# Eight PSUM banks dealt out anew among dense sums, down products and norms in an inference step

## The chip, the cores and the metric

The kernel runs on one core of a Trainium2 chip. The metric is the device time of one execution in microseconds; the median of three executions before the change is 4295.14 (4291.89 to 4296.32). A separate execution was profiled, and its trace is what is read below.

## The reference

One inference step of a small hybrid diffusion backbone, width 1024, on 1280 token positions: 256 of one request's context (x_prompt) and 1024 of a noisy sample (x_sample). There are two trunk layers, each a mixer and an MLP, with a residual add behind each:

```
x = x + gate * mixer(rmsnorm(x) * (1 + scale) + shift)     # scale, shift, gate: linear in silu(c)
x = x + gate * (relu(h @ w1) ** 2) @ w2                    # h = rmsnorm(x) * (1 + scale) + shift
```

The even layer's mixer is a gated DeltaNet beside a short gated convolution; the odd layer's is a windowed attention with grouped queries and sink logits beside an RWKV-7 time mixing. Both mixers start with dense projections of h (some followed by a convolution of three taps) and end with a dense output projection. After the two layers a last RMSNorm gives y_prompt and y_sample; the final DeltaNet and RWKV states and the key and value cache of the context are outputs too.

## The kernel before

**Layout and precision.** x lies transposed in SBUF, eight tiles of 128 features by 1280 positions. Positions are worked in three chunks, `CHUNKS`, in this order: 512, 512 and 256 columns. Every float32 operand of a dense product is split into a high and a low part (`split`, L243 to L247, on ScalarE, VectorE or GpSimd), and a product is the sum of three matmuls: high by high, high by low, low by high. `dense_mm` (to L271) makes one dense sum of 128 output features by up to 512 positions: eight blocks of 128 inputs by three matmuls, 24 in all, added up in one PSUM tile.

**PSUM.** There are eight banks. `set_ps` (L99) closes the pools that are open and opens one pool for each keyword, in the order of the keywords, with as many tiles as the number says; `ps_t` (L104) takes a tile of 128x512 float32, one bank, from the pool of that name. `ps_d()` is a tile of pd (dense sums), `ps_m()` one of pm. A pool goes round its banks: a new tile waits until the last reader of the tile that had its bank is done. Pools are opened at five places:

- L138, for the load of x, the modulation vectors and the first norm
- L587, for the even mixer (pd dense sums, pm small products, pg and pr the DeltaNet's)
- L1293, for RWKV and attention (pc, pp, pi, pa, po), which has no pd and is not touched
- L1895, for the even mixer's output, the first MLP and the odd mixer's projections
- L1905, for the odd mixer's output, the second MLP and the final norm

**Who uses pd.** At the places with three pools: `load_x` (L456), which transposes x (L151) four blocks to a tile and copies them out on VectorE (L472) and ScalarE (L470); the MLP's up sums; the odd mixer's projections (`conv_block` and L1202 to L1250), emptied by ScalarE (L571 and L572 in `conv_block`, L1205 behind it); the output projections (L1054, L1859), emptied by VectorE into x; `final`, which transposes the result four blocks to a tile and empties it at L542 on VectorE.

**Who uses pn and pm.** A norm takes a pn tile for the sums of squares of a chunk (`rstd_chunk`: squares by ScalarE at L419 or GpSimd at L417, sums by TensorE at L421, read by VectorE at L424) and one to spread the result over the partitions (L440), which VectorE reads at L445; activations at L448 and L451 on ScalarE follow. `mod_vec` takes tiles for the modulation vectors, whose partial sums VectorE adds at L344 and L346. pm also holds the MLP's down products.

**The MLP** (`mlp`, L475) goes through 16 groups of 256 hidden features. `up` makes for each of the group's two blocks a dense sum (L271), a ReLU from PSUM on ScalarE (L495), a square (L496) and a split. `down` makes eight output blocks of six matmuls (L506 to L508) and adds them into x on VectorE (L509). Within a group:

```
h0 = up(a0, n0)        # 512 columns: two dense sums
h1 = up(a1, n1)        # 512 columns: two dense sums
down(h0, a0, n0, s0)
h2 = up(a2, n2)        # 256 columns: two dense sums
```

**What sets the order.** The Tile framework plans the program: each engine gets a static list of instructions, drawn up from program order, priorities (the sums of squares and the spreading of a norm stand under a high priority) and a simulated timeline. On the chip each engine works through its list in order, and an instruction that waits holds back all behind it on that engine, the transfers that the engine issues included.

Of the kernel before, what the change touches and what calls it, by code (L numbers as in the profile page):

```python
# [85 lines left out]
def tile_kernel(ctx, tc, I, O):  # L86
# [7 lines left out]
    def pool(es, name, bufs, **kw):  # L94
        return es.enter_context(tc.tile_pool(name=name, bufs=bufs, reuse_waits="tile", **kw))
# [3 lines left out]
    def set_ps(**banks):  # L99
        ps_es.close()  # L100
        for nm, n in banks.items():
            state[nm] = pool(ps_es, nm, n, space=PSUM)
# [30 lines left out]
    def open_t5(es, bufs, sq=0, **kw):  # L133
        state["t5"] = pool(es, "t5", bufs, **kw)
        if sq:
            state["sq"] = pool(es, "sq", sq, **kw)

    set_ps(pd=3, pm=3, pn=2)  # L138


    cnames, _, cnames64, _ = const_arrays()
# [95 lines left out]
    def open_w(es, nraw, nhl):  # L237
        state["raw"] = pool(es, "wraw", nraw)
        state["whl"] = pool(es, "whl", nhl)
# [338 lines left out]
    def even_mixer(hs):  # L578
# [5 lines left out]
        mid.update(o=sp_o, s=sp_s)  # L584
        tap = lambda k, j: vec["gdn_conv"][:, k * 12 + j:k * 12 + j + 1]
        stap = lambda k, j: vec["sc_conv"][:, k * 4 + j:k * 4 + j + 1]
        set_ps(pd=2, pm=1, pg=2, pr=3)  # L587
        with ExitStack() as es:
            cp = pool(es, "conv", 1, side="right")
            mp = pool(es, "modp", 2, side="right")  # L590
# [1300 lines left out]
    xes.close()  # L1891

    even_mixer(hs)

    set_ps(pd=3, pm=3, pn=2)  # L1895
    open_t5(tes, 4, 3, side="right")
    xt = new_x(xes)
    unspill_x(xt)
# [3 lines left out]
    mlp(wes, 0, xt, hs, mod_gate(0, 1), [(), ()] + [(1, 512 * n) for n in range(12)])  # L1902
    odd_mixer(xt, hs, hes, xes, wes)

    set_ps(pd=3, pm=3, pn=2)  # L1905
    open_w(wes, 2, 2)
    hs = new_h(hes)
    open_t5(tes, 4, 2, side="right")
# [42 lines left out]
```

## Time and profile before

| what | value |
|---|---|
| median of three runs | 4295.14 us (4291.89 to 4296.32) |
| profiled execution, its own time | 4296.43 us |
| its span | 4294.6 us |
| TensorE busy | 3989.5 us, 93% of the span |
| VectorE busy | 2240.2 us, 52% |
| ScalarE busy | 1269.8 us, 30% |
| GpSimd busy | 1279.6 us, 30% |
| matmuls | 27995 |

The span is from the first to the last instruction in the trace; the profiled execution's own time has a little around it. Busy time is the time in which an engine has an instruction in work. An idle time before an instruction is put down to the event that released it, and a TensorE instruction's length overlaps with that of the next, since matmuls are pipelined: the distance between two starts is what one costs.

The stages follow one another: load, modulation and first norm up to 120 us; the even mixer to about 905, with its output behind it; the first MLP from 982 to about 1905; norm and projections of the odd mixer to 2113; RWKV and attention from 2114 to 3195; the odd mixer's output from 3198 to 3347; the second MLP from 3348; the final norm to the end.

### The profile page before, as it was taken

What the parts mean: (1) busy time and instruction counts of PE and PEld (TensorE: products, weight loads), DVE (VectorE), ACT (ScalarE), POOL (GpSimd) and SP (SyncE); (2) the same over time, 40 slices, a digit from 0 to 9 for tenths busy, and PEclk for the clock granted to TensorE, in tenths of its full rate; (3) what the DMA queues carried; (4) which work ended last, traced back from release to release, by engine and by line L of the source; (5) the groups of instructions that cost most, each with busy time, mean ns of one, the idle gap of its engine ahead of it and who ended that gap; (6) DMA issues with size and microseconds to landing.
All of it is one profiled execution on the core that took longest, in us unless ns stands there. A gap on an engine that the chain in (4) does not pass through costs nothing.

```text
span 4294.6 us, 70066 instructions
## 1 busy us (share of the span) xinstructions
PE 3989.5 (93%) x27995; PEld 3293.4 (77%) x27995; DVE 2240.2 (52%) x4724; ACT 1269.8 (30%) x2691; POOL 1279.6 (30%) x1139
## 2 busy tenths in 40 slices
PE   7889989998999999999889889999859999999999
PEld 4777778787888888887667667776648888888888
DVE  2467676545455555453365577777631433333333
ACT  3554543222111111133223234444321311111111
POOL 1544542223222333232432231212022323223321
PEclk8989999999999999999989889999879999999999
DMA  5323332432122222125466543333241111111111
GB/s 198 103 82 102 95 97 73 128 124 72 54 75 71 73 77 74 47 87 188 144 211 183 140 104 90 94 91 86 53 144 47 30 40 40 40 40 40 40 35 54
DMA packets 437957, 382.98 MB, mean 89 GB/s; under 512 B 125684, under 2 KB 373503, under 8 KB 437503
## 3 DMA queue, kind: packets, MB, share of 16 engines
q1 hardware_dynamic: 403727, 310.34, 24.7%
q10 hardware_dynamic: 33904, 68.17, 4.8%
q8 instruction: 220, 3.60, 0.4%
q14 instruction: 106, 0.87, 0.1%
HBM read 290.31 MB, written 88.08 MB: 88 GB/s over the span
## 4 chain that ended last, share of the span: by engine, by line
PE 75%; DVE 11%; DMA 7%; issue 3%; ACT 2%; POOL 2%; SPq 1%; ACTq 0%; DVEq 0%; POOLq 0%
PE pd L271 31%; PE pm L506 7%; PE pm L507 7%; PE pm L508 7%; PE pd L280 3%; PE pn L421 2%; PE po L1453 1%; PE pa L1271 1%; PE pp L1583 1%; PE pa L1442 1%; DVE stmp L842 1%; DVE sub L844 1%; DMA modw<-in_mod_w_dram 1%; DMA hst<-sp_h 1%; DMA vg<-sp_k 1%
## 5 line engine op out<-in xcount | busy, mean ns | idle before, releaser
L271 PE MATMUL pd<-hhi,whl 128*128 128x512 f32 (+1 forms) x5376 | 1527.7, 364 | 45.4 <-ACT hhi L243 23.4
L271 PEld LDWEIGHTS pd<-hhi,whl 128*128 128x128 f32 x5376 | 966.8, 191 | 200.1 <-ACT hhi L243 24.7
L271 PE MATMUL pd<-hlo,whl 128*128 128x512 f32 (+1 forms) x2688 | 980.1, 365 | 10.9 <-POOL hlo L247 9.2
L509 DVE SCALAR_TENSOR_TENSOR x<-pm,mods,x 128x512 f32<-128x512 f32 (+1 forms) x768 | 502.4, 660 | 751.1 <-PE pm L508 751.0
L247 POOL TENSOR_TENSOR whl<-raw,whl 128x1024 fp32r<-128x1024 f32 (+2 forms) x203 | 469.6, 2323 | 605.0 <-ACT whl L243 605.0
L271 PEld LDWEIGHTS pd<-hlo,whl 128*128 128x128 f32 x2688 | 514.9, 192 | 90.8 <-POOL hlo L247 11.2
L506 PE MATMUL pm<-hh,whl 128*128 128x512 f32 (+1 forms) x1536 | 546.9, 356 | 0.0
L507 PE MATMUL pm<-hl,whl 128*128 128x512 f32 (+1 forms) x1536 | 545.1, 355 | 0.0
L508 PE MATMUL pm<-hh,whl 128*128 128x512 f32 (+1 forms) x1536 | 544.1, 354 | 0.0
L495 ACT ACTIVATE t<-pd 128x512 f32<-128x512 f32 (+1 forms) x192 | 100.9, 527 | 1311.9 <-PE pd L271 1311.9
L247 POOL TENSOR_TENSOR hl<-t,hh 128x512 fp32r<-128x512 f32 (+1 forms) x192 | 216.2, 1126 | 822.8 <-DVE hh L245 806.0
L506 PEld LDWEIGHTS pm<-hh,whl 128*128 128x128 f32 x1536 | 289.4, 188 | 44.5
L507 PEld LDWEIGHTS pm<-hl,whl 128*128 128x128 f32 x1536 | 289.8, 189 | 43.6
L508 PEld LDWEIGHTS pm<-hh,whl 128*128 128x128 f32 x1536 | 289.9, 189 | 41.6
L245 DVE CAST hh<-t 128x512 fp32r<-128x512 f32 (+1 forms) x192 | 166.6, 869 | 236.1 <-ACT t L496 235.9
L243 ACT ACTIVATE whl<-raw 128x1024 fp32r<-128x1024 f32 (+2 forms) x203 | 201.8, 1011 | 154.6 <-PE pm L508 75.0
L357 POOL TENSOR_TENSOR acc<-acc,modw 128x512 f32<-128x512 f32 x112 | 149.2, 1332 | 135.1 <-ACT modw L353 116.6
L346 DVE SCALAR_TENSOR_TENSOR acc<-modw,scp,acc 128x512 f32<-128x512 f32 x168 | 129.0, 804 | 3.8 <-DMA modw<-in_mod_w_dram 3.8
L1271 PE MATMUL pa<-hst,whl 128*128 128x512 f32 (+1 forms) x432 | 120.9, 380 | 9.2 <-DMA hst<-sp_h 8.7
L353 ACT ACTIVATE modw<-modw,scp 128x256 f32<-128x256 f32 x224 | 112.7, 506 | 54.6 <-DMA modw<-in_mod_w_dram 49.6
L421 PEld LDWEIGHTS pn<-cst,sq 128*128 128x128 f32 x800 | 109.3, 209 | 8.2 <-issue 2.5
L280 PE MATMUL pd<-hhi,whl 128*128 128x512 f32 (+1 forms) x384 | 111.5, 366 | 2.5 <-DVE xr L1015 1.6
(387 smaller groups left out, 6019.1 us busy)
## 6 DMA issues: line engine op xcount, KB each, us to landing
raw<-in_mlp_w_dram SPq DMA_DIRECT2D x128, 512.0 KB
modw<-in_mod_w_dram SPq DMA_DIRECT2D x112, 256.0 KB
hst<-sp_h ACTq DMA_DIRECT2D x48, 512.0 KB
modw<-in_mod_w_dram SPq DMA_DIRECT2D x128, 128.0 KB
rkk<-sp_r SPq DMA_DIRECT2D x40, 384.0 KB
raw<-in_ev_w_in_dram SPq DMA_DIRECT2D x28, 512.0 KB
x_dram<-x SPq DMA_DIRECT2D x16, 640.0 KB
x<-x_dram ACTq DMA_DIRECT2D x32, 256.0 KB
```

What stands on the lines that cost most here:

```text
L243: A.activation(out=hi, in_=src, func=AF.Copy)
L245: V.tensor_copy(out=hi, in_=src)
L247: G.tensor_tensor(out=lo, in0=src, in1=hi.bitcast(F32), op=ALU.subtract)
L271: paced(PE.matmul(ps[:, :N], w, x[:, t0:t0 + N], start=(n + i == 0), stop=(n == KB - 1 and i == 2)), N / 2400)
L280: paced(PE.matmul(ps[:, :N], w, x[:, t0:t0 + N], start=(kb + i == 0), stop=(kb == 3 and i == 2)), N / 2400)
L357: G.tensor_tensor(out=acc, in0=acc, in1=w, op=ALU.add)
L421: PE.matmul(pst[:, 2 * t:2 * t + 2], sq[:, t * P:(t + 1) * P], C["ones"][:, 0:2], start=(kb == 0 and t == 0), stop=(kb == KB - 1 and t == ...
L506: PE.matmul(ps[:, :N], wh, hh[:, b, :N], start=(b == 0), stop=False)
L507: PE.matmul(ps[:, :N], wh, hl[:, b, :N], start=False, stop=False)
L508: PE.matmul(ps[:, :N], wl, hh[:, b, :N], start=False, stop=(b == 1))
L509: V.scalar_tensor_tensor(out=xt[db][:, t0:t0 + N], in0=ps[:, :N], scalar=gate[:, db, s:s + 1], in1=xt[db][:, t0:t0 + N], op0=ALU.mult, op1 ...
L1271: burst([(lambda w_=w_, i=i, w=w, h=h: PE.matmul(st["ps"][w_][:, :N], st["w"][w_][:, w, kb, :], x[:, h, :N], start=(kb + i == 0), stop=(kb ...
```

## The change

At four of the five places the pools are opened in another order, and so lie in other banks. At three of them pd has two banks where it had three, and pn three where it had two; pm keeps three. At L587 no pool's number of banks changes.

| place | pool | banks before | banks after |
|---|---|---|---|
| L138, L1895, L1905 | pd | 0, 1, 2 | 6, 7 |
| | pm | 3, 4, 5 | 3, 4, 5 |
| | pn | 6, 7 | 0, 1, 2 |
| L587 | pd | 0, 1 | 6, 7 |
| | pm | 2 | 5 |
| | pg | 3, 4 | 3, 4 |
| | pr | 5, 6, 7 | 0, 1, 2 |

```diff
--- before.py
+++ after.py
@@ -135,7 +135,7 @@
         if sq:
             state["sq"] = pool(es, "sq", sq, **kw)
 
-    set_ps(pd=3, pm=3, pn=2)
+    set_ps(pn=3, pm=3, pd=2)
 
 
     cnames, _, cnames64, _ = const_arrays()
@@ -584,7 +584,7 @@
         mid.update(o=sp_o, s=sp_s)
         tap = lambda k, j: vec["gdn_conv"][:, k * 12 + j:k * 12 + j + 1]
         stap = lambda k, j: vec["sc_conv"][:, k * 4 + j:k * 4 + j + 1]
-        set_ps(pd=2, pm=1, pg=2, pr=3)
+        set_ps(pr=3, pg=2, pm=1, pd=2)
         with ExitStack() as es:
             cp = pool(es, "conv", 1, side="right")
             mp = pool(es, "modp", 2, side="right")
@@ -1892,7 +1892,7 @@
 
     even_mixer(hs)
 
-    set_ps(pd=3, pm=3, pn=2)
+    set_ps(pn=3, pm=3, pd=2)
     open_t5(tes, 4, 3, side="right")
     xt = new_x(xes)
     unspill_x(xt)
@@ -1902,7 +1902,7 @@
     mlp(wes, 0, xt, hs, mod_gate(0, 1), [(), ()] + [(1, 512 * n) for n in range(12)])
     odd_mixer(xt, hs, hes, xes, wes)
 
-    set_ps(pd=3, pm=3, pn=2)
+    set_ps(pn=3, pm=3, pd=2)
     open_w(wes, 2, 2)
     hs = new_h(hes)
     open_t5(tes, 4, 2, side="right")
```

## Rows read from the trace of the kernel before

**Rows 1.** The page, parts 1 and 4: busy time by engine, and the chain

```profile
PE 3989.5 (93%) x27995; PEld 3293.4 (77%) x27995; DVE 2240.2 (52%) x4724; ACT 1269.8 (30%) x2691; POOL 1279.6 (30%) x1139
...
PE pd L271 31%; PE pm L506 7%; PE pm L507 7%; PE pm L508 7%; PE pd L280 3%; PE pn L421 2%; PE po L1453 1%; PE pa L1271 1%; PE pp L1583 1%; PE pa L1442 1%; DVE stmp L842 1%; DVE sub L844 1%; DMA modw<-in_mod_w_dram 1%; DMA hst<-sp_h 1%; DMA 
```

**Rows 2.** Busy time by stage: window, length, busy us (instructions) per engine, PEclk, DMA

```profile
960.00:1830.00 870.00, 856.91 (x4523) 725.86 (x4522) 474.34 (x730) 169.01 (x272) 261.43 (x161) 0.99 0.23 68
3348.00:4250.00 902.00, 894.76 (x4643) 763.34 (x4643) 338.02 (x495) 179.48 (x291) 271.04 (x173) 0.99 0.12 37
...
2114.00:3195.00 1081.00, 933.87 (x10762) 714.26 (x10762) 700.59 (x1909) 389.99 (x1006) 259.17 (x374) 0.90 0.45 122
```

**Rows 3.** The page, part 5: the ReLU that empties a dense sum

```profile
L495 ACT ACTIVATE t<-pd 128x512 f32<-128x512 f32 (+1 forms) x192 | 100.9, 527 | 1311.9 <-PE pd L271 1311.9
```

**Rows 4.** What TensorE waits for: us in total, times, longest

```profile
PE pd L271 <- ACT t L495: 18.4, 2, 12.2
...
PE pp L1543 <- DMA lin<-sp_l: 13.6, 1, 13.6
```

**Rows 5.** TensorE's timeline, first MLP's start: start, us, instruction [idle before <-releaser]

```profile
995.26 0.40 PE L271 MATMUL pd<-hlo,whl 128*128 128x512 f32 x1
...
996.66 0.40 PE L271 MATMUL pd<-hlo,whl 128*128 128x512 f32 x1
...
1012.75 0.80 PE L271 MATMUL pd<-hhi,whl 128*128 128x512 f32 x1 [12.23 <-ACT t L495]
```

**Rows 6.** ScalarE's timeline at the same place

```profile
1007.09 0.91 ACT L451 ACTIVATE hhi<-t,mods 128x256 fp32r<-128x256 f32 x2 [18.58 <-DVE t L445]
...
1012.13 1.06 ACT L495 ACTIVATE t<-pd 128x512 f32<-128x512 f32 x2
...
1013.39 0.59 ACT L495 ACTIVATE t<-pd 128x512 f32<-128x512 f32 x1
```

**Rows 7.** VectorE's timeline at the same place

```profile
1006.58 1.65 DVE L445 SCALAR_TENSOR_TENSOR t<-x,ab,pn 128x256 f32<-128x256 f32 x4
```

**Rows 8.** Windows of 5 us at the same place (the clock stands after POOL)

```profile
1010.00:1015.00 5.00, 2.25 (x5) 1.82 (x6) 2.58 (x7) 4.39 (x11) 1.57 (x2) 0.50 0.00 0
1015.00:1020.00 5.00, 5.00 (x16) 3.90 (x15) 1.88 (x2) 0.53 (x2) 3.91 (x3) 0.64 0.00 0
```

**Rows 9.** Timeline of all engines, start of the second MLP

```profile
3367.51 0.93 ACT L419 ACTIVATE sq<-x 128x256 f32<-128x256 f32 x2 [0.75 <-PE pn L421]
...
3371.40 0.16 DVE L424 TENSOR_SCALAR ms<-pn 128x2 f32<-128x2 f32 x1 [5.21 <-PE pn L421]
...
3379.31 0.80 PE L271 MATMUL pd<-hhi,whl 128*128 128x512 f32 x1 [6.22 <-ACT t L495]
```

**Rows 10.** TensorE's timeline, start of the odd mixer's projections

```profile
1945.81 0.79 PE L271 MATMUL pd<-hhi,whl 128*128 128x512 f32 x1 [1.39 <-ACT lr L572]
...
1973.70 0.28 PE L271 MATMUL pd<-hlo,whl 128*128 128x256 f32 x1
...
1975.84 0.28 PE L271 MATMUL pd<-hlo,whl 128*128 128x256 f32 x1
...
1978.58 0.50 PE L271 MATMUL pd<-hhi,whl 128*128 128x512 f32 x1 [2.00 <-ACT lr L572]
```

**Rows 11.** TensorE's timeline, start of the odd mixer's output

```profile
3230.09 0.50 PE L271 MATMUL pd<-hlo,whl 128*128 128x512 f32 x1 [2.00 <-POOL hlo L247]
...
3232.52 0.41 PE L271 MATMUL pd<-hlo,whl 128*128 128x256 f32 x1
...
3234.53 0.92 PE L271 MATMUL pd<-hhi,whl 128*128 128x256 f32 x2
```

**Rows 12.** TensorE's timeline, the final norm's transposes

```profile
4275.97 10.21 PE L151 MATMUL pd<-cst,x 128*128 128x128 f32 x56
```

**Rows 13.** VectorE's timeline, the same place

```profile
4281.42 6.94 DVE L542 SCALAR_TENSOR_TENSOR ob<-pd,rs,gfin 128x512 f32<-128x512 f32 x10 [0.16 <-PE pd L151]
```

**Rows 14.** TensorE's timeline, the load of x

```profile
13.69 1.97 PE L151 MATMUL pd<-cst,xs 128*128 128x128 f32 x8 [4.02 <-ACT x L470]
```

## The prediction, as put on record

> **What bounds the kernel now.** I read the page's busy shares and its chain first, then busy time by stage, then TensorE's waits, then the timelines of every place where a pool's bank count could be felt. TensorE is busy 93% of the span, and the chain that ended last is led by the dense sums of L271 with 31% and by the MLP's down products with three times 7% [rows 1]. By stage it is clearer: in the body of the first MLP TensorE is busy 856.9 of 870 us, in the second 894.8 of 902, both at clock 0.99, while between 2114 and 3195 (RWKV and attention) it is busy 933.9 of 1081 [rows 2]. So TensorE time lost inside or just ahead of an MLP moves the end one for one; nothing later is idle enough to give it back.
>
> The next question is whether the number of banks of the dense sums, pd, is ever the limit. ScalarE runs the ReLU that empties a pd bank 192 times, 527 ns each, and has 1311.9 us of idle time in front of it, all of it waiting for the sum itself [rows 3]: in the steady body the reader of a bank waits for TensorE and not the other way. But TensorE waits 18.4 us, twice in all, for that ReLU, and 12.2 of it at one place [rows 4]. Those two places, and the starts of the other stages that use pd, are where the third bank does something.
>
> **The change part by part.** The diff has two kinds of line. At L587 the four pools keep their counts and change places. At L138, L1895 and L1905 the places change too, but the counts with them: pd goes from three banks to two, the norms' pn from two to three, the down products' pm keeps three.
>
> *Places.* I cost them at 0: every sum has a bank to itself in either order, and no row gives one bank another price than the next. What a price would make is worked out as a rival.
>
> *pn from two to three.* The norm's sums come from squares which ScalarE makes only as x and the squares' buffer come free; at the second MLP the square at 3367.51 had waited for TensorE's pn matmuls, not for a bank [rows 9]. I cost it at 0.
>
> *pd from three to two in the steady bodies.* A sum of 512 columns is 24 matmuls; 995.26 to 996.66 is six of them in 1.40 us, 0.233 each, 5.6 us a sum [rows 5]. A sum of 256 columns is 24 at 0.119 (18 in 2.14 us between 1973.70 and 1975.84), 2.9 us [rows 10]. With two banks, sum k+2 needs the evacuation of sum k, and has the whole of sum k+1 as cover: 2.9 us at least against a ReLU of 0.53. Cost 0. If that cover were gone, each of the 192 would show.
>
> *Start of the first MLP.* TensorE finishes three sums of 512 and then idles 12.23 us, to 1012.75, for the ReLU [rows 5]; three ReLUs follow one another at once, two from 1012.13 and one at 1013.39 [rows 6]. ScalarE is late, because it works in a written order: activations of the norm's last chunk from 1007.09 stand ahead of them, and these had waited 18.58 us for VectorE's L445 [rows 6], which came up only at 1006.58, behind modulation adds [rows 7]. The stall ends by that order and not by TensorE. With two banks the third sum can't be open; TensorE stops after the second, the stall still ends near 1012.7, and the third sum comes behind it: +5.6 us. The floor is 0 (if the shorter queue on TensorE or another order lets the norm finish sooner), the ceiling 5.8 (the sum plus its share of norm matmuls). The clock is down to 0.50 before the stall's end and 0.64 in 1015 to 1020 [rows 8]; it would be in either kernel, so I add nothing.
>
> *Start of the second MLP.* Same picture, smaller: TensorE idles 6.22 us before 3379.31, for the ReLU, again after three sums [rows 9]. Here VectorE's L424 had waited 5.21 us for pn matmuls that stand in TensorE's queue among the matmuls of the third sum [rows 9]. Take that sum away and the norm's last chunk may come up to half a sum earlier, the stall with it. I take +2.8, half a sum; 0 if all of it comes earlier, 5.6 if nothing.
>
> *Start of the odd mixer's projections.* Three sums are done (512, 512, 256 columns) before TensorE waits at 1945.81 for the evacuation of the first by L572 [rows 10]. The third sum would run after 1945.8: +2.9. At 1978.58 TensorE waits 2.00 us again for L572 [rows 10], where up to 2.0 of it can be absorbed: 0.9 to 2.9. I take +2. It isn't hidden later: the next stage begins with a wait of 13.6 us for a load of what this stage spilled [rows 4], which moves along.
>
> *Start of the odd mixer's output.* Three sums advance together as their inputs arrive, the last of them, for all three, at 3230.09 after a wait of 2.00; they end within a microsecond of 3234.5 [rows 11]. With two banks the one of 256 columns runs whole behind the others, 2.9 us, less the six matmuls that it has after the last arrival even now (the first at 3232.52, the last two at 3234.53 [rows 11]), 0.7: +2.2 (1.8 to 2.9).
>
> *The end.* From 4275.97 fourteen transposed tiles take TensorE 10.21 us, 0.73 a tile [rows 12]; VectorE empties ten in 6.94, 0.69 each [rows 13]. With three banks both run on. With two, the round of one bank is 0.73 to fill and 0.69 to empty, and by my estimate 0.18 for two handovers (VectorE's wait of 0.16 for TensorE in [rows 13] is one at its longest): 1.6, 0.8 a tile, so +0.07 on each of 17 tiles, 1.2, and one tile less is done ahead. I take +1.5, between 0 and 2.7 (1.2, one whole tile, and a handover twice as long on every second).
>
> *The load at the start.* TensorE waits 4.02 us before 13.69 for ScalarE's copy, after three tiles; two tiles take 1.97 us [rows 14]. One tile fewer ahead: +0.7, between 0 (covered by the modulation loads that follow) and 1.5.
>
> The sum is 0.7 + 5.6 + 2 + 2.2 + 2.8 + 1.5 = +14.8 us, with 2.7 and 21.4 as the sums of all lower and upper ends. The profiled execution took 4296.43 (span 4294.6), 1.3 above the median of the runs; 4296.4 + 14.8 = 4311.2, and by the median 4295.1 + 14.8 = 4309.9. I forecast 4310.
>
> **The rivals.** *The third bank was worth nothing at the MLPs.* The order on each engine is planned anew; if the norm's last chunk comes sooner by what the missing sum leaves free, both MLP starts cost nothing and 6.4 us remain: 4301.5. For it: at the second MLP the norm's own sums stand behind the third sum [rows 9]. Against it: at the first, VectorE is what is late [rows 6, 7]. The case that the pools only change places in effect belongs here too, at 4295.
>
> *Faster: the ReLU moves ahead of the norm's last chunk in ScalarE's queue.* A plan that has no free bank can want the evacuation earlier. If it stands ahead of the activations of 1007.09, TensorE goes on with a fourth sum and with down products through the stall: up to 12.2 and 6.2 us come back in place of +8.4, with +6.4 elsewhere: 4295.1 - 18.4 + 6.4 = 4283. It decides from the point where the ReLU is ahead in both; with the first alone it is 4295.1 - 12.2 + 6.4 + 2.8 = 4292. Against it: ScalarE was idle for 18.58 us at that very place [rows 6], so the planner did not foresee the idle time, and the norm comes earlier in the program.
>
> *Faster: the place of the bank matters.* If dense matmuls ran faster in banks 6 and 7, one ns on each of the 4608 matmuls of the ReLU's 192 sums [rows 3] is 4.6 us; 2.4% of 0.233 us, a step that would matter, 26 us, 4269. No row speaks for it.
>
> *Slower by much: two banks do not cover the evacuation.* If each of the 192 ReLUs were exposed, 100.9 us would be added [rows 3], 4396. The row speaks against it: ScalarE waits for the sums. The Trainium skill, "Perfetto Trace Analysis", section "Optimization Strategy", says that the same gap repeating on the engine that should be saturated can mean that there is too little PSUM for the next tile; by that rule two banks would show such gaps, and in the bodies of before, with three, there are none to speak of: 13 us idle in 870 [rows 2]. A milder form is the clock: 1% of it over the 1772 us of both bodies is 17.7 us, 4313. The Trainium skill, "TensorE: Matmul & The Clock Gate", section "A second HAM failure mode: psum-queue depth-cycling", tells of a kernel that cycles PSUM banks with short idles in between and whose clock then swings; the trace does not agree so far, since the bodies cycle banks at 0.99 [rows 2].
>
> **How the numbers follow.** The forecast gets 0.60, its own range 4298 to 4316. No cost at the MLPs gets 0.22, the earlier ReLU 0.08, the bank's place 0.03, two banks too few or a worse plan in the stages that hang on chains 0.07. The range reaches from 4288 (the faster case in part) to 4322. A change of 0.2%, 8.6 us, is about what a measurement of this kernel can tell from none. Of the forecast's 0.60 about 0.10 lies under 4303.7; of the second case nearly all. Faster 0.11, within 0.2% 0.30, slower 0.59.
>
> **What would show it.** Right: at both MLP starts TensorE stops after two sums, its wait for L495 in the list of waits grows from 18.4 us to about 27 or more, with the stall's end at its old place in the first; one sum fewer ahead of the waits at the projections, the output and the load; bodies with the same matmul spacing and no idle time at L271. Wrong: three sums' worth of work before the stalls, an L495 ahead of L451, a spacing other than 0.233 us in the bodies, or a difference that grows between 2114 and 3195, where I expect none beyond what came before.

## The result: 1.1% slower, and where the profile after shows it

The changed kernel takes 4333.82 us (4328.25 to 4341.81, five runs) against 4291.89 of the kernel before in as many, ratio 1.0106 (95% interval 1.0088 to 1.0124). The ratio gives 45 us, the two medians lie 42 us apart. The prediction was 4310, or +14.8 us, with a range to 4322: the direction is right, the size is three times too small. By the two profiled executions the span grew from 4294.6 to 4332.0, 37.4 us.

The page of the changed kernel, parts 1 and 5, answers to [rows 1, 3]: TensorE has as many matmuls and 34 us more of busy time, and the ReLU still waits for its sums.

```profile
PE 4023.9 (93%) x27995; PEld 3314.4 (77%) x27995; DVE 2248.6 (52%) x4724; ACT 1269.6 (29%) x2691; POOL 1284.7 (30%) x1139
...
L495 ACT ACTIVATE t<-pd 128x512 f32<-128x512 f32 (+1 forms) x192 | 100.8, 526 | 1321.1 <-PE pd L271 1321.1
```

Three stages of the changed kernel (window, length, busy us and instructions of PE, PEld, DVE, ACT, POOL, then the granted clock, DMA share, GB/s): 870 us of the first MLP, the RWKV and attention stage from its first matmul to the first of the output, 902 us of the second MLP, to be laid beside [rows 2].

```profile
964.00:1834.00 870.00, 855.11 (x4495) 723.19 (x4494) 472.22 (x729) 168.08 (x270) 262.40 (x162) 0.99 0.23 68
2132.00:3234.00 1102.00, 956.38 (x10763) 729.49 (x10763) 705.43 (x1908) 391.02 (x1005) 255.76 (x362) 0.88 0.43 118
3386.00:4288.00 902.00, 893.81 (x4638) 762.95 (x4637) 338.41 (x495) 178.07 (x287) 269.09 (x172) 0.99 0.12 37
```

The same RWKV and attention stage in the kernel before:

```profile
2127.00:3199.00 1072.00, 934.09 (x10763) 714.45 (x10764) 699.92 (x1908) 389.99 (x1005) 255.85 (x362) 0.90 0.44 121
```

The bodies of the MLPs are as full as before (855.1 and 893.8 us, 856.9 and 894.8 in [rows 2]) at the same clock, with two dense banks. The stage between them, whose own pools and matmuls the diff does not touch, is 1102 us long in place of 1072, at 0.88 in place of 0.90 of the clock, for the same 10763 matmuls. Cutting both traces at the same matmuls gives the whole account:

| from, to | before, us | after, us | difference | prediction's terms |
|---|---|---|---|---|
| start, first product of the even mixer (L706) | 90.6 | 86.3 | -4.3 | +0.7 |
| to the last matmul of its output (L280) | 889.6 | 893.2 | +3.6 | 0 |
| to the first down product of the first MLP | 40.9 | 42.5 | +1.6 | +5.6 |
| to its last | 901.4 | 904.6 | +3.2 | 0 |
| to the first matmul of the RWKV stage (L1543) | 204.5 | 205.1 | +0.6 | +2 |
| to the first matmul of the odd mixer's output | 1071.8 | 1101.8 | +30.0 | 0 |
| to the first down product of the second MLP | 188.3 | 191.3 | +3.0 | +5.0 |
| to its last | 884.9 | 884.4 | -0.5 | 0 |
| to the end | 22.6 | 22.8 | +0.2 | +1.5 |

The row to L280 and the first row are no finding (see e1 below). Thirty of the 37 us lie in one row. In it, the traces part at the preparation of unit 6 (the stage works eight units, numbered from 0, two directions for each of four pairs of heads; `prep` makes a unit's operands while the unit before runs its recurrence). Cut into three, from the stage's start to the preparation of unit 5, from there to that of unit 6, and from there to the output, the stage looks like this before:

```profile
2127.00:2674.00 547.00, 489.55 (x4697) 374.15 (x4697) 347.98 (x874) 186.40 (x459) 149.32 (x207) 0.89 0.53 148
2674.00:2807.50 133.50, 124.98 (x1615) 94.89 (x1614) 106.49 (x314) 59.00 (x154) 34.26 (x50) 0.94 0.37 93
2807.50:3198.80 391.30, 319.36 (x4455) 245.21 (x4453) 245.46 (x722) 144.38 (x392) 72.08 (x105) 0.90 0.35 93
```

and after:

```profile
2131.70:2676.60 544.90, 496.31 (x4701) 375.88 (x4701) 349.25 (x882) 186.04 (x459) 149.32 (x207) 0.88 0.53 149
2676.60:2843.50 166.90, 144.12 (x1851) 109.20 (x1850) 124.58 (x363) 65.29 (x171) 34.55 (x50) 0.92 0.32 80
2843.50:3233.50 390.00, 315.72 (x4217) 244.22 (x4212) 231.60 (x665) 139.19 (x375) 71.43 (x104) 0.87 0.34 91
```

The first and the last part are as long as before, to about 2 us; the middle is 166.9 in place of 133.5. The first matmul of unit 6's preparation, in TensorE's timeline before and after:

```profile
2807.50 0.70 PE L1543 MATMUL pp<-lin,ups 64*128 64x256 f32 x2
```

```profile
2843.55 0.70 PE L1543 MATMUL pp<-lin,ups 64*128 64x256 f32 x2
```

In the experiments' table, "preparation" is this start, counted from the stage's first matmul (at 2127.0 before, at 2131.7 after). It needs ups, three small weight tiles loaded once for a pair. SP's queue of the kernel before around that load (issue time, length of issue):

```profile
2805.44 0.34 SPq L1527 DMA_DIRECT2D ups<-in_rwkv_w_up_dram  x1
...
2811.71 0.58 SPq L1539 DMA_DIRECT2D lin<-sp_l  x1
...
2831.18 0.32 SPq L1615 DMA_DIRECT2D rbi<-sub  x1
```

and of the changed kernel:

```profile
2825.09 0.33 SPq L1615 DMA_DIRECT2D rbi<-sub  x1
2827.76 7.29 SPq L1618 DMA_DIRECT2D Gm<-rbi  x13
...
2836.44 4.58 SPq L1618 DMA_DIRECT2D Gm<-rbi  x7
...
2841.54 0.43 SPq L1527 DMA_DIRECT2D ups<-in_rwkv_w_up_dram  x1
...
2848.83 0.58 SPq L1539 DMA_DIRECT2D lin<-sp_l  x1
```

SP works through its list in order. Before, the ups loads stand ahead of rbi (L1615), the exchange that brings a unit's inverted blocks back; after, they stand behind it and behind the twenty transfers of L1618, which wait for rbi. They go out at 2841.5 in place of 2805.4. The ups tile has two buffers, so this load also waits for the last reader of the pair before last, L1830 in `finish`. Its matmuls from 2780 on (median durations, then first and last start), before:

```profile
L1830 PE MATMUL pa<-vg,ups x4: 379/379/483, 2791.7 to 2805.0; 128*128 128x256 f32 x4
```

after:

```profile
L1830 PE MATMUL pa<-vg,ups x6: 379/432/796, 2785.9 to 2829.1; 128*128 128x256 f32 x6
```

The last reader starts at 2805.0 before, 0.4 us ahead of the load, and at 2829.1 after: 24 us late itself (19 counted from the stage's start), and the load then stands behind the exchange for 12 more. Part of why the reader is late shows in VectorE's list. The finish goes through five parts of 256 positions, and its steps stand among those of unit 5's inversion (L1612 and L1613 by turns, from 2785.74 before and from 2792.78 after). The first step of the fourth part stands behind one such pair before,

```profile
2786.68 0.41 DVE L1803 TENSOR_REDUCE mean<-Yt 128x4 f32<-128x256 f32 x1
```

and behind seven after:

```profile
2799.32 0.41 DVE L1803 TENSOR_REDUCE mean<-Yt 128x4 f32<-128x256 f32 x1
```

### The profile page after: what moved, and what is told of

Its sections match the earlier page's. It is cut to its first block, busy times and chain, and to the rows that moved or that the text cites. A ratio compares the mean times of both kernels' runs of the same rounds, so it can differ in the third digit from the quotient of the medians.

```text
span 4332.0 us, 70058 instructions
## 1 busy us (share of the span) xinstructions
PE 4023.9 (93%) x27995; PEld 3314.4 (77%) x27995; DVE 2248.6 (52%) x4724; ACT 1269.6 (29%) x2691; POOL 1284.7 (30%) x1139
## 4 chain that ended last, share of the span: by engine, by line
PE 74%; DVE 11%; DMA 8%; issue 3%; POOL 2%; ACT 1%; SPq 1%; ACTq 0%; POOLq 0%; DVEq 0%
PE pd L271 32%; PE pm L506 7%; PE pm L507 7%; PE pm L508 7%; PE pn L421 2%; PE pd L280 2%; PE pa L1271 2%; PE po L1453 1%; PE pp L1583 1%; DVE sub L844 1%; DMA modw<-in_mod_w_dram 1%; PE pa L1442 1%; DVE stmp L1612 1%; DVE sub L1613 1%; DMA vg<-sp_k 1%
## 5 line engine op out<-in xcount | busy, mean ns | idle before, releaser
L495 ACT ACTIVATE t<-pd 128x512 f32<-128x512 f32 (+1 forms) x192 | 100.8, 526 | 1321.1 <-PE pd L271 1321.1
L280 PE MATMUL pd<-hhi,whl 128*128 128x512 f32 (+1 forms) x384 | 113.6, 369 | 3.3 <-DVE xr L1015 1.5
```

The source lines that it names most:

```text
L280: paced(PE.matmul(ps[:, :N], w, x[:, t0:t0 + N], start=(kb + i == 0), stop=(kb == 3 and i == 2)), N / 2400)
```

## The experiments

Each was timed in five rounds against the kernel before on the same chip. "Stage" is the time from the stage's first matmul to the first of the output, as in the table, in the run's own profiled execution; "written order" is the list that the planner draws up for each engine, compared line by line with the kernel before. The expectations of e1 to e8 count the stage to its own last matmul, some 17 us sooner: 1055 before, 1084 in the changed kernel. By that count e1 took 1055.3, e2 1062.6, e3 1060.6, e4 1056.4, e5 1061.1, e6 1088.9, e7 1062.9 and e8 1115.6.

| run | ratio (95% interval) | stage, us | preparation, us into the stage |
|---|---|---|---|
| before | 1 | 1071.8 | 680.5 |
| changed kernel | 1.0106 (1.0088 to 1.0124) | 1101.8 | 711.8 |
| e1 places alone | 1.0005 (0.9991 to 1.0019) | 1072.5 | 678.3 |
| e2 L587 undone | 1.0076 (1.0061 to 1.0091) | 1080.4 | 680.9 |
| e3 L1895 new | 1.0030 (1.0015 to 1.0045) | 1078.0 | 680.9 |
| e4 L1895 counts | 0.9981 (0.9970 to 0.9993) | 1073.0 | 696.0 |
| e5 loads ahead | 1.0023 (1.0006 to 1.0040) | 1078.4 | 682.1 |
| e6 two dense banks, one idle | 1.0114 (1.0095 to 1.0133) | 1105.7 | 718.8 |
| e7 new counts, another order | 1.0033 (1.0018 to 1.0049) | 1080.1 | 683.7 |
| e8 exchange on ScalarE | 1.0182 (1.0160 to 1.0203) | 1133.0 | 758.9 |
| e9 L1905 counts | 1.0014 (0.9995 to 1.0033) | 1072.0 | 678.5 |
| e10 L138 counts | 1.0005 (0.9991 to 1.0020) | 1074.3 | 684.1 |
| e11 four dense banks at L1905 | 1.0012 (0.9998 to 1.0025) | 1070.7 | 681.0 |
| e12 e4 and e11 | 1.0005 (0.9989 to 1.0021) | 1069.4 | 693.4 |
| e13 changed, ups split | 1.0025 (1.0010 to 1.0040) | 1072.5 | 665.4 |
| e14 before, ups split | 0.9968 (0.9954 to 0.9983) | 1055.1 | 648.1 |
| e15 e12, ups split | 1.0029 (1.0015 to 1.0044) | 1077.6 | 660.8 |

**e1, the places alone.**

```diff
-    set_ps(pd=3, pm=3, pn=2)            # L138, L1895, L1905
+    set_ps(pn=2, pm=3, pd=3)
-        set_ps(pd=2, pm=1, pg=2, pr=3)  # L587
+        set_ps(pr=3, pg=2, pm=1, pd=2)
```

> All four lines with the pools opened in the new order, but with the counts of before (pd 3, pm 3, pn 2): only the banks' places differ; the written order of every engine is that of before. Replanning theory (the new counts gave the stage of RWKV and attention another written order, and that order costs the time): no change, ratio 1.000 within 0.002, stage from the first L1543 to the last matmul 1055 us as before. Rival, the places matter (a dense sum runs slower in banks 6 and 7, or stages collide in their banks): a good part of the 42 us shows, ratio 1.005 to 1.010, and the matmul spacing in the MLP differs from 0.233 us.

No change: the interval holds 1, and the RWKV stage is 0.7 us away from that of before. With the same written order, the even mixer is 5.5 us longer and the start 3.3 shorter: so much can differ between two profiled executions in those two stages, and the -4.3 and +3.6 in the table above are no finding. With the counts of before, the bank in which a sum lies costs nothing that can be measured. It does not follow that the counts alone do the rest: with new counts, the order in which the pools are opened helps to set the written order (e7).

**e2, the changed kernel with L587 undone.**

```diff
-        set_ps(pr=3, pg=2, pm=1, pd=2)
+        set_ps(pd=2, pm=1, pg=2, pr=3)
```

> The changed kernel with L587 alone set back to the old order: the counts at L138, L1895 and L1905 are the new ones, the even mixer's pools lie as before. The written order of the RWKV and attention stage is then within 20 lines of that of before. Replanning theory: that stage takes 1055 us again instead of 1084, and only the direct costs of two dense banks remain, some 8 us (ratio 1.001 to 1.003). Rival, the two banks or three norm banks themselves hurt that stage (late release, other arrival of its inputs): it stays near 1084 us, ratio 1.008 to 1.011.

The stage fell to 1080.4, but not to the 1071.8 of before, though its written order is that of before but for some 20 lines; the 8.6 us that are left were not expected. The whole stayed high for another reason that I had not seen. TensorE's timeline at the even mixer's first product:

```profile
105.98 0.61 PE L706 MATMUL pd<-hhi,whl 128*32 128x512 f32 x1 [24.18 <-DVE t L445]
```

The first dense sum of the even mixer now lies in a bank of the norm's pool and waits 24.18 us for VectorE's L445, the norm's reader: the first product comes at 106.0 in place of 90.6. So places do matter where one set of pools hands over to the next, if they overlap badly; in the changed kernel and in e1 all four lines moved together and the handover stayed as it was.

**e3 and e4, the L1895 line, whole and in its counts.** One after the other, against the kernel before:

```diff
-    set_ps(pd=3, pm=3, pn=2)
+    set_ps(pn=3, pm=3, pd=2)    # e3
+    set_ps(pd=2, pm=3, pn=3)    # e4
```

> The kernel before with the L1895 line alone changed, counts and places (pn 3, pm 3, pd 2): the first MLP and the odd mixer's projections have two dense banks. The written order of the RWKV stage differs from that of before in 18 lines. Replanning theory: the stage takes 1055 us; first MLP and projections cost 3 to 8 us more, ratio 1.0005 to 1.002. Rival: the two dense banks ahead of the RWKV stage make it late: 20 us and more, ratio above 1.005.

> The kernel before with the new counts at L1895 alone but the pools in the old order (pd 2, pm 3, pn 3): the same number of banks for the same stages as in the run with the whole new L1895 line, yet the written order of the RWKV stage differs from that of before in some 3950 lines. Replanning theory: first MLP and projections cost 3 to 8 us as there, and the RWKV stage takes a time of its own, some tens of us away from 1055 in either direction (likelier longer, 1065 to 1090). Rival, only the counts matter: the same time as the run with the whole L1895 line, within 4 us.

The two have the same counts in the same stages and differ by 0.5% (1.0030 and 0.9981, intervals apart), so the counts alone don't set the time. e4's order of the RWKV stage differs from that of before in 3950 lines and its stage takes 1073.0: many changed lines need not cost anything. That the new order would cost some tens of us, as expected for e4, was wrong; e4 was faster than the kernel before. e3 cost more than was expected, 6 us of it in the stage, whose order it leaves as before but for 18 lines. e4's preparation of unit 6 comes 15.5 us later than before and costs the stage nothing, so a late preparation is not by itself a longer stage.

**e5, the changed kernel with the ups loads at high priority.**

```diff
-                for i, src in enumerate(...):
-                    SY.dma_start(out=ups[:, i], in_=src[:, b * P:(b + 1) * P])
+                with tc.high_priority():
+                    for i, src in enumerate(...):
+                        SY.dma_start(out=ups[:, i], in_=src[:, b * P:(b + 1) * P])
```

> The changed kernel, all banks as changed, with one edit in the RWKV stage: the three loads of ups in prep (L1527) stand at high priority. In the changed kernel's written order of SP the ups loads of the last head pair stand behind the exchange of the unit before (L1615 and twenty L1618); with the edit they stand 17 rows ahead of it, as in the kernel before. Replanning theory, narrowed to this place (the preparation of unit 6 came 20 us late for its queue's order): the stage takes 1055 to 1065 us in place of 1084, the whole is 4298 to 4312, ratio 1.001 to 1.005. Rival, the counts themselves cost the stage: it stays near 1084, ratio about 1.010.

With every bank as in the changed kernel, the stage takes 1078.4 and the whole is 0.8% faster than the changed kernel by the two ratios. SP's queue in this run (L1528 and L1616 are the L1527 and L1615 of before):

```profile
2809.68 0.34 SPq L1528 DMA_DIRECT2D ups<-in_rwkv_w_up_dram  x1
...
2835.70 0.32 SPq L1616 DMA_DIRECT2D rbi<-sub  x1
```

The loads are ahead of the exchange again, as expected, and stage and whole lie in the expected ranges. But the edit moved more than the loads: on VectorE, ScalarE and SP together, the stage's order in this trace differs from that of the changed kernel in 4529 lines and from that of before in 212 (lines missing and lines added, of some 3900). It is nearly the order of before, so this run prices that whole order and not the loads alone.

**e6, two dense banks, the eighth bank idle.**

```diff
-    set_ps(pd=3, pm=3, pn=2)    # L138, L1895, L1905
+    set_ps(pd=2, pm=3, pn=2)
```

> The kernel before with two dense banks at L138, L1895 and L1905 and nothing else: pd 2, pm 3, pn 2 in the old order, one bank lies idle. In SP's written order the ups loads of the last pair stand behind the exchange, as in the changed kernel. Replanning theory, narrowed: the stage takes 1078 to 1090 us, ratio 1.007 to 1.012. Rival, the third norm bank is what hurts: the stage is near 1055, ratio 1.001 to 1.003.

1105.7 us, as slow as the changed kernel, with the loads behind the exchange:

```profile
2836.97 0.33 SPq L1615 DMA_DIRECT2D rbi<-sub  x1
...
2853.59 0.43 SPq L1527 DMA_DIRECT2D ups<-in_rwkv_w_up_dram  x1
```

The third norm bank is not what hurts. By the same count the stage's order is that of the changed kernel but for 394 lines.

**e7, the new counts in another order.**

```diff
-    set_ps(pd=3, pm=3, pn=2)    # L138, L1905
+    set_ps(pd=2, pm=3, pn=3)
-    set_ps(pd=3, pm=3, pn=2)    # L1895
+    set_ps(pn=3, pm=3, pd=2)
```

> All three counts as in the changed kernel (pd 2, pm 3, pn 3), but with the pools in the old order at L138, L587 and L1905 and in the new order at L1895. The written order of the RWKV stage differs from that of before in some 300 lines and from that of the changed kernel in 3000, with the ups loads ahead of the exchange. Replanning theory: the stage takes 1055 to 1063 us and the whole 8 to 16 us more than before, ratio 1.002 to 1.004. Rival, the counts cost the stage: 1084, ratio about 1.010.

All three counts of the changed kernel, another written order (671 lines from that of before, 3858 from that of the changed kernel), and the stage is 1080.1, the whole 14 us over before. With e5 this is the plainest answer: the same banks cost 0.2 to 0.3% under one order and 1.1% under another.

**e8, the exchange's way back on ScalarE, in the changed kernel.**

```diff
-            SY.dma_start(out=bi.rearrange("q c j i -> (q c) j i"), in_=sub)
+            A.dma_start(out=bi.rearrange("q c j i -> (q c) j i"), in_=sub)
-                    SY.dma_start(out=blk(grp[c0][1], qd), in_=...)
+                    A.dma_start(out=blk(grp[c0][1], qd), in_=...)
```

> The changed kernel with the exchange's way back (L1615, L1618: 21 transfers for each of eight units) issued by ScalarE in place of SP. If it is the waiting exchange at the head of SP's queue that makes the preparation late, the stage loses its 20 us at the last pair: 1055 to 1070 us, though ScalarE now stands still while it waits for the inversion and issues, which may cost some of it again. If the order on the other engines holds the preparation back, not the queue, the stage stays at 1080 or more.

Worse, 1133 us: the preparation comes 758.9 us into the stage, later still. With the exchange out of SP's queue, the loads go out at 2891.7, 0.5 us after the last reader of ups, L1830 at 2891.2: here the late finish alone holds them. That ScalarE loses more while it waits and issues than SP gains is a reading, not shown. By itself this run does not tell queue and order apart.

**e9 to e12, direct prices, and a version with more dense banks.**

```diff
-    set_ps(pd=3, pm=3, pn=2)
+    set_ps(pd=2, pm=3, pn=3)    # e9 at L1905, e10 at L138, e12 at L1895
+    set_ps(pd=4, pm=2, pn=2)    # e11 and e12 at L1905
```

> The kernel before with the new counts at L1905 alone (pd 2, pm 3, pn 3, old order): only the odd mixer's output, the second MLP and the final norm have two dense banks, and the written order differs only there (243 lines on TensorE). This prices the direct cost. By the terms of the prediction 2.2 + 2.8 + 1.5 = +6.5 us, ratio 1.0015; by the changed kernel's trace, in which the way from the output's first matmul to the end is 2.7 us longer, +3, ratio 1.0006. Rival: the third bank was worth nothing here, 0 within 1 us.

> The kernel before with the new counts at L138 alone (old order): load and first norm have two dense banks and three norm banks. The even mixer's written order changes in some 320 lines, the RWKV stage's in 20. By the prediction's term +0.7 us; by the changed kernel's trace the even mixer's first product comes 4 us earlier and its end 0.8 us earlier: between -5 and +1, ratio 0.999 to 1.000. Replanning theory: the RWKV stage stays within 2 us of 1072 (first L1543 to first matmul of the output).

> The kernel before with four dense banks, two for down products and two for norms at L1905 (pd 4, pm 2, pn 2). If a dense bank is worth one sum ahead of the stall at the second MLP's start, a fourth one gives a sum back: TensorE does four sums ahead of the wait for L495, -3 to -6 us, ratio 0.9985 to 0.9995. Rival: two banks for the down products hold TensorE back in the body (eight down sums of 1.4 us in a row, each emptied by a VectorE step of 0.75 us), and the body is longer than 902 us by 5 us or more.

> New counts at L1895 alone (as in the run that was faster than the kernel before, ratio 0.9981) and four dense banks at L1905 (pd 4, pm 2, pn 2). The order up to the odd mixer's output is that of the faster run. If the fourth bank pays at L1905, the two gains add: ratio 0.996 to 0.998. If it does not, this is no faster than the run with the L1895 counts alone, 0.998 or more.

e9 and e10 leave the RWKV stage within 2.5 us of before and their ratios hold 1 in the interval: 0.14% and 0.05% are the best estimates, 6 and 2 us, but neither is shown. In e11's profile the first down product of the second MLP comes 7.4 us earlier, counted from the output's first matmul (180.9 us in place of 188.3), and the body from there is 7.5 us longer (892.4 in place of 884.9): the way from the output's first matmul to the last down product takes 1073.3 us, before 1073.2. The fourth dense bank brings the sums forward and the two banks of the down products give that back, both theories at once. e12 is no faster than e4; its interval neither shows nor excludes a gain of e4's size beside e11's.

**e13 to e15, the ups tile split.**

```diff
-                ups = tp.tile([P, 3, P], F32, tag="ups", name="ups", bufs=2)
+                ups = tp.tile([P, 2, P], F32, tag="ups", name="ups", bufs=2)   # read by prep
+                gup = tp.tile([P, P], F32, tag="gup", name="gup", bufs=2)      # read by finish, L1830
```

> The changed kernel with the ups tile split in two: the two weights that prep reads (L1543) in a tile of their own, the one that finish reads (L1830) in another, two buffers each, so that the loads for the preparation of a new head pair no longer wait for the finish of the pair before last. In the changed kernel that wait ended at 2829 and the loads went out at 2842; in the kernel before 2805 and 2805. Theory of the shared buffer: the preparation of unit 6 starts near 2810 or sooner, the stage takes 1065 to 1080 us in place of 1101.8, the whole 4300 to 4310, ratio 1.001 to 1.004. Rival: the finish of the pair itself, late in the written order, is what costs; then the stage stays above 1090, ratio 1.007 or more.

> The kernel before with the same split of ups. Theory of the shared buffer: here the loads went out 0.4 us after the finish and ahead of the exchange, so that little was lost: the stage 1065 to 1073 us, ratio 0.998 to 1.000, and the difference to the changed kernel with the split is the direct cost of the banks, 5 to 12 us. Rival (a lucky order): any new order is worse, the stage 1078 or more.

> New counts at L1895, four dense banks at L1905, and the split of ups. In the run without the split the loads went out right behind the finish of the pair, and the preparation of unit 6 began at 2816. Theory of the shared buffer: that preparation may begin earlier, 0 to 8 us gained, ratio 0.996 to 1.000. Rival: the loads were not what ended last there, ratio 0.999 to 1.002.

The changed kernel with the split, e13, has the stage back at 1072.5, and the preparation starts so (L1544 is L1543 of before):

```profile
2795.74 0.70 PE L1544 MATMUL pp<-lin,ups 64*128 64x256 f32 x2
```

The kernel before with the split is the fastest of all, 0.9968 (0.9954 to 0.9983): it beats both kernels. Its two loads for prep go out 240 us earlier than before, and the preparation of unit 6 starts 32 us earlier in the stage:

```profile
2566.25 0.43 SPq L1528 DMA_DIRECT2D ups<-in_rwkv_w_up_dram  x1
2566.73 0.43 SPq L1528 DMA_DIRECT2D ups<-in_rwkv_a_up_dram  x1
```

```profile
2772.37 0.70 PE L1544 MATMUL pp<-lin,ups 64*128 64x256 f32 x2
```

Its stage of 1055.1 is under the 1065 to 1073 expected. The shared buffer seems to have cost the kernel before something too, though the split also changed the order (4436 lines). For the changed kernel this matters: with the split in both, its stage is still 17.4 us longer (1072.5 against 1055.1) and its time 0.57% or 24 us more, where 5 to 12 us were expected. Of the 30 us in the stage the split takes 12.6 away, about the 12 for which the loads stood behind the exchange. And e15 has an early preparation (660.8) and a stage of 1077.6, longer than e12 without the split, and a ratio of 1.0029 that neither its expectation nor the rival had: an early preparation is not enough, and why that order is slower is open.

## Why the prediction was wrong, point by point

**The step that failed** is the last sentence's "a difference that grows between 2114 and 3195, where I expect none beyond what came before", and with it the sum, which has no term for that stage. I saw that the order is planned anew and used it only at the MLPs' starts; for the rest "a worse plan in the stages that hang on chains" shared a chance of 0.07 with another case. The runs put a 30 us term there: with the new pools the planner wrote the stage in another order, in which the finish of a head pair and the loads of the next pair come later. By what steps a count moves the planner's times was not looked at. The same counts under two other orders, e5 and e7, cost 1.0023 and 1.0033; another count with the same late loads, e6, costs 1.0114; places alone, with an unchanged order, cost nothing that shows, e1.

**How much is shown.** Sorted by the stage's order, as the traces have it on VectorE, ScalarE and SP, and by pd at L1895, the stage's lengths in us fall into groups:

| order of the stage | pd 3 at L1895 | pd 2 at L1895 |
|---|---|---|
| that of before (3 to 23 lines differ; e5 212, e7 671) | before 1071.8, e1 1072.5, e9 1072.0, e10 1074.3, e11 1070.7 | e2 1080.4, e3 1078.0, e5 1078.4, e7 1080.1 |
| that of the changed kernel (e6 394) | | changed kernel 1101.8, e6 1105.7 |
| e4's (e12 7) | | e4 1073.0, e12 1069.4 |
| with ups split (e13 and e14 differ in 614) | e14 1055.1 | e13 1072.5 |

e8 and e15 have orders of their own. So the order is what makes most of the 30 us: at the same counts, the order of the changed kernel takes 21 to 24 us more than that of before (e2, e5, e7). The other 6 to 9 us stay when the order is that of before and pd at L1895 is 2; they, too, lie in a stage whose own pools no edit touches, and their cause is open. What in the order costs the 21 to 24 us is in part argued. In the changed kernel and e6, the two with the long stage, the ups loads stand behind the exchange; in e2, e3, e4, e5, e7, e9, e10 and e12, which all have some or all of the new counts, the loads go out 0.4 us after the last L1830 starts and ahead of the exchange, and the stage takes 1069.4 to 1080.4. But each of these edits makes a new order on the other engines as well, so the late finish, the late loads and the rest of the order can't be priced one by one; e4 (late preparation, no cost) and e15 (early preparation, no gain) show that the rest counts.

**The direct terms.** The changed kernel's trace without that stage is 7.4 us longer, where the sum said 14.8; the timed ratios of e5 and e7 come to 9.9 and 14.2 us (2.6 to 21 by their intervals), with 7 to 8 us of it in the stage. Two single traces are a coarse measure of terms of this size. The medians over all profiled runs with three and with two dense banks at the place are a better one (e11, e12 and e15 have four at L1905 and are left out of the last two rows):

| from, to | foreseen | before to after | three banks: median (range, runs) | two banks | difference |
|---|---|---|---|---|---|
| last L280 to the last down product of the first MLP | +5.6 | +4.8 | 942.2 (941.8 to 942.4, 6) | 944.3 (943.3 to 947.5, 11) | +2.1 |
| to the first matmul of the RWKV stage | +2 | +0.6 | 204.2 (203.4 to 204.6, 6) | 205.3 (204.5 to 206.8, 11) | +1.1 |
| first matmul of the odd mixer's output to the first down product of the second MLP | +5.0 | +3.0 | 186.3 (182.9 to 188.4, 6) | 191.7 (189.6 to 193.3, 8) | +5.4 |
| last down product of the second MLP to the end | +1.5 | +0.2 | 22.5 (21.6 to 23.3, 6) | 23.7 (22.8 to 24.1, 8) | +1.2 |

Together +9.8 of 14.1: the terms of the second half of the kernel were right, those of the first were too large. One by one:

- First MLP's start, +5.6 foreseen, +2.1 by the medians. (The changed kernel's trace has +1.6 up to the first down product and +3.2 in the body behind it; of the other runs with two banks only e6 has such a body.) TensorE did stop after two sums in place of three, but the stall did not end at its old place. Timeline of all engines in the changed kernel:

```profile
1001.16 1.65 DVE L445 SCALAR_TENSOR_TENSOR t<-x,ab,pn 128x256 f32<-128x256 f32 x4
...
1008.79 1.05 ACT L495 ACTIVATE t<-pd 128x512 f32<-128x512 f32 x2
...
1009.42 0.79 PE L271 MATMUL pd<-hhi,whl 128*128 128x512 f32 x1 [12.63 <-ACT t L495]
```

VectorE's L445 comes at 1001.16, 5.4 us earlier than in [rows 7], among the modulation adds and no longer behind them all, so that the stall ends at 1009.42 in place of 1012.75 [rows 5]. The first rival's "at the first, VectorE is what is late" named the right place and drew the wrong conclusion: the planner moved that work.

- The wait for L495 did not grow to "about 27 or more": it is 18.9 us, 18.4 in [rows 4].

```profile
PE pd L271 <- ACT t L495: 18.9, 2, 12.6
...
PE pp L1543 <- DMA lin<-sp_l: 12.5, 1, 12.5
```

- Second MLP's start, with the output before it, +5.0 foreseen, +5.4 by the medians. Two sums ahead in place of three, and a stall of the same length as in [rows 9], since the norm's last chunk did come up sooner, as the step said. From the MLP's first matmul, here before and after,

```profile
3348.38 0.48 PE L271 MATMUL pd<-hhi,whl 128*128 128x512 f32 x1
```

```profile
3384.36 0.64 PE L271 MATMUL pd<-hhi,whl 128*128 128x512 f32 x1
```

to the stall's end it is 30.9 us before [rows 9] and 27.7 after: 3.2 of the missing sum's 5.6 us come back, about the half that the step took. The stall's end after:

```profile
3412.08 0.80 PE L271 MATMUL pd<-hhi,whl 128*128 128x512 f32 x1 [6.22 <-ACT t L495]
```

- Projections, +2 foreseen, +1.1 by the medians. TensorE stops one sum earlier, as foreseen, and waits longer for L572 than in [rows 10]:

```profile
1949.94 0.58 PE L271 MATMUL pd<-hhi,whl 128*128 128x256 f32 x1 [8.59 <-ACT lr L572]
```

  In e3, the first matmul of the RWKV stage is 3.6 us late, and the stage 6 us longer on top.
- The end, +1.5 foreseen, +1.2 by the medians. TensorE's transposes in the changed kernel, eighteen tiles of four:

```profile
4312.75 4.40 PE L151 MATMUL pd<-cst,x 128*128 128x128 f32 x20
4317.34 1.32 PE L151 MATMUL pd<-cst,x 128*128 128x128 f32 x8 [0.18 <-DVE ob L542]
4318.84 8.16 PE L151 MATMUL pd<-cst,x 128*128 128x128 f32 x44 [0.18 <-DVE ob L542]
```

  That is 14.25 us from the first to the end, 0.79 a tile, where before it was 0.73 [rows 12], seventeen tiles in all: the 0.8 and the one tile less ahead were right. In these two traces TensorE ends 1.4 us later, counted from the last down product, and little of it shows at the end, because before the last two copies had to wait for an output transfer anyway:

```profile
4289.20 1.41 DVE L542 SCALAR_TENSOR_TENSOR ob<-pd,rs,gfin 128x512 f32<-128x512 f32 x2 [0.84 <-DMA out_dram<-ob]
```

- The load, +0.7 foreseen, -4.3 found to the even mixer's first product; by e1 that lies within what two profiles differ by, and e10, which changes L138 alone, shows no difference in time (1.0005).

**What held.** Hardly more idle time in the bodies at two dense banks (14.9 and 8.2 us, 13.1 and 7.2 before), against the rival that would have cost 101 us, and the clock at 0.99 in both MLPs, against its milder form. The Trainium skill, "TensorE: Matmul & The Clock Gate", section "A second HAM failure mode: psum-queue depth-cycling", tells of a kernel that cycles PSUM banks with short idles in between and whose clock swings; the trace does not agree for two banks either, at 0.99. And the place of the bank has no price that can be measured (e1).

## What to carry to other kernels

A buffer count in a planned kernel is an input of the planner, not only a resource: before forecasting, compare the written order of every stage behind the edit, above all of those that hang on chains, and look in the queues' order for transfers that have moved behind a wait. Where one tile holds operands with different last readers, its next load waits for the slowest of them; try tiles of their own. Here that paid in two kernels (e13 against the changed kernel, e14 against the kernel before) and not in a third (e15 against e12). And price an edit under two or three orders before calling the difference its cost: here the same counts cost 0.2%, 0.3% or 1.1%.

## What the runs showed that I had not expected

Kernels whose orders of the RWKV stage differ in thousands of lines and whose work is the same took 1055 to 1106 us for it, and the kernel before, at 1072, is not the best of them. A pool set that is only half turned round (e2) made the first sum of a stage wait 24.18 us for the reader of another pool's bank.
